# High part of the attention probabilities from a second exponential of the scores, not from a copy

## The chip, the cores and the metric

The kernel runs on one core of a Trainium2 chip. The time is device time in microseconds (us) for one execution, on inputs and outputs in device memory. A core has five engines that work at the same time, each on its own queue of instructions, in order: TensorE (PE, matmuls; PEld are its weight loads), VectorE (DVE), ScalarE (ACT, functions such as the exponential, and copies), GpSimd (POOL) and SyncE (SP, which starts most of the transfers). Matmul results land in PSUM, eight banks of 128 x 512 floats; POOL's operands here lie in SBUF.

## The reference

One layer of a decoder trunk over L = 1040 tokens (16 meta tokens and 1024 of the sequence), width 1024. An input projection feeds four mixers (pooling, attention, two convolutions), their outputs are gated, added and projected. Attention, which the change touches, has 8 heads, keys of 96 and values of 64:

```python
h = rms_norm(h_res, pre_norm_g[i])
z = h @ w_in[i]
...
s = jnp.einsum('bqhd,bkhd->bhqk', qb, k).astype(jnp.float32)
s = jnp.where(k_pos[None, :] <= q_pos[:, None], s, -jnp.inf)
p = jax.nn.softmax(s, axis=-1).astype(v.dtype)
return jnp.einsum('bhqk,bkhd->bqhd', p, v)
...
m = (gts[:, :, 0] * y_a + gts[:, :, 1] * y_b + gts[:, :, 2] * y_c + gts[:, :, 3] * y_d)
h_res = h_res + rms_norm(m @ w_o[i], post_norm_g[i])
```

## The kernel before

**Three-term products.** A float32 product is made of three matmuls in the format fp32r: each operand is split into a high part (the value rounded to fp32r) and a low part (the rest), and high x high, high x low and low x high are added in PSUM. The helper `split` (line 498) makes both parts: ACT copies the source into the high part, POOL subtracts the high part from the source to get the low one.

**Stages.** The first stage (to about 638 us) makes the input projection and the mixers' inputs. The second (638 to 838 us) is attention, mixed with the output products of the three other branches, which the code calls fills. The third makes the attention branch's output product and the last projection.

**Attention.** `attend(h, c)` (line 1507) works on one head `h` and one half `c` of the queries (512 of them). It runs over tiles of 128 keys, 4 full ones for `c = 0` and 8 for `c = 1`, and a last one of 16 keys. A tile covers 512 queries, or at the diagonal 400, 272, 144 and 16; over all heads 48 tiles have 512 columns, and 16 each have 400, 272 and 144. For each full tile:

- three matmuls into `s`, a PSUM bank of the tag `s`; five banks serve all users of that tag. Their rows read `ps_s<-qt,kt`;
- at the diagonal DVE adds a mask to the bank (`ps_s<-ps_s,maskT`);
- ACT takes the exponential into `p32` in SBUF, of which there are three buffers (`p<-ps_s`; a row maximum is already folded into the scores by four extra rows of the keys and queries);
- `split` makes `pt`, high and low side by side, four buffers (`pt<-p` on ACT, `pt<-p,pt` on POOL);
- three matmuls with the values add to `po`, the one bank `ps_o`: high x high, then the low part, then the third with the values' low part, which is put off by some tiles (`thirds`). A `pt` buffer is free after its third matmul.

The tile of 16 keys goes another way: ACT copies `p32` twice into `pz`, and POOL subtracts. At the end of a half ACT copies `po` to `ol` in SBUF (two buffers, one for a head); a new head's `ol` can be written when both products `op<-ol,rb` on DVE have read the one before the last. `rb` holds the reciprocal row sums, brought round by three small transfers; in the last head TensorE makes them by transposes (`ps_s<-ident,ol` and `ps_s<-ident,lcp`). POOL then multiplies with a gate (`op<-op,smg`), and `split` makes `boM` from it.

Two other users of the five banks and of TensorE stand between: the row maxima of a later half (`ps_s<-kt,qt`, masked with `maskS` and reduced on DVE into `mxs`), and the fills, six matmuls `ps_y<-bo,whl` each, of which DVE multiplies the result with a gate (`th<-th,ps_y`) and adds it up (`m<-m,th`, by turns on POOL).

**What sets the order.** Engine calls in the code don't issue anything. `Plan.record` notes each with its operands and a cost from a formula, and `Plan.flush` (line 364) runs a list scheduler over them: at each step an engine takes the noted instruction of lowest priority number that is ready and for which buffers are free. It then issues all instructions in the order found, from line 362, which is why every row of the profile names that one line. So the order on each engine, and which buffer a tile gets, is fixed ahead of time. A change in one instruction's operands or cost moves others in the stage.

Of the kernel before, what the change touches and what calls it, by code (L numbers as in the profile page):

```python
# [24 lines left out]
AF = mybir.ActivationFunctionType  # L25
# [8 lines left out]
NM = 16  # L34
# [38 lines left out]
def f(ap):  # L73
    return ap.bitcast(F32)
# [397 lines left out]
def trunk_kernel(ctx, tc, a):  # L472
    nc = tc.nc
    plan = Plan(nc)
    PE, ACT, DVE, POOL, SP = (plan.engine(e) for e in ("PE", "ACT", "DVE", "POOL", "SP"))
# [10 lines left out]
    def copy(out, in_, scale=1.0):  # L486
        ACT.activation(out, in_, AF.Copy, scale=scale)

    def sub(eng, out, x, y):
        eng.tensor_tensor(out, x, y, op=ALU.subtract)  # L490

    def add(eng, out, x, y):
        eng.tensor_tensor(out, x, y, op=ALU.add)
# [4 lines left out]
    def split(hi, lo, src, eng=None):  # L498
        copy(hi, src)
        sub(eng or POOL, lo, src, f(hi))  # L500
# [55 lines left out]
    def bank(tag="x"):  # L556

        return psum.tile([P, 512], F32, tag=tag, bufs=2 if tag == "x" else 1, name=f"ps_{tag}")
# [948 lines left out]
    def attend(h, c):  # L1507

        q_, k_, v_ = qt[h, c], kt[h % 2], vt[h % 2]
        po = bank("o")  # L1510
        nj = 4 * c + 5
        thirds = []

        def rest(last=False):
            PE.matmul(*thirds.pop(0), start=False, stop=last, skip_group_check=True)

        for j in range(nj):
            lo_ = max(512 * c, P * j - NM)
            n = 512 * (c + 1) - lo_
            kn = P if j < nj - 1 else NM  # L1520
            ks = slice(P * j, P * j + kn)
            qs = slice(512 - n, 512)
            s = bank("s")[:kn, :n]
            PE.matmul(s, k_[:NA, 0, ks], q_[:NA, 0, qs], start=True, stop=False)
            PE.matmul(s, k_[:QK, 0, ks], q_[:QK, 1, qs], start=False, stop=False)
            PE.matmul(s, k_[:QK, 1, ks], q_[:QK, 0, qs], start=False, stop=True)
            d0 = P * j - NM
            dl, dh = max(d0, 512 * c, 0), min(d0 + P, 512 * (c + 1))
            if dh > dl:
                sd = s[:, dl - lo_:dh - lo_]  # L1530
                add(DVE, sd, sd, maskT[:kn, dl - d0:dh - d0])
            p32 = at.tile([P, 512], F32, tag="p32", bufs=3, name="p32")[:kn, :n]
            ACT.activation(p32, s, AF.Exp)
            o = po[:, lo_ - 512 * c:]
            if kn == NM:
                x = pz[(2 * h + c) % 3]
                copy(x[:NM], p32)
                copy(x[64:], p32)
                sub(POOL, x[32:32 + NM], p32, f(x[:NM]))
                PE.matmul(o, vs[h % 2][:, c], x, start=False, stop=False, skip_group_check=True)  # L1540
                rest(last=True)
            else:
                pt_ = at.tile([P, 2, 512], F32R, tag="pt", bufs=4, name="pt")[:, :, :n]
                split(pt_[:, 0], pt_[:, 1], p32)
                PE.matmul(o, v_[:, j, :P], pt_[:, 0], start=(j == 0), stop=False, skip_group_check=True)
                if j == nj - 2:
                    rest()
                PE.matmul(o, v_[:, j, :P], pt_[:, 1], start=False, stop=False, skip_group_check=True)
                thirds.append((o[:64], v_[:, j, P:], pt_[:, 0]))
                if j < nj - 4 or j == nj - 2:  # L1550
                    rest()
            yield
        if c == 0:
            ol[h] = at.tile([P, 2, 512], F32, tag="ol", bufs=2, name="ol")
        with plan.late(500 if h == H - 1 else 0):
            copy(ol[h][:, c], po)
# [114 lines left out]
    for i, (h, c) in enumerate(seq):  # L1671
        with plan.behind() if i else nullcontext():
            if i + 2 < len(seq):
                load_q(*seq[i + 2])
            if c == 0 and h + 1 < H:
                load_kv(h + 1)
                if i == 0:
                    with plan.behind():
                        load_v(1)
            if h % 2 and c == int(h < H - 1):  # L1680
                smg[h] = at.tile([P, NT], F32, tag="smg", name="smg")
                ld(smg[h], z_dram[f"mg{h // 2}"])
        for j, _ in enumerate(attend(h, c)):
            if c and j == 4 and h + 2 < H:
                load_k(h + 2, 0, CUT)
            units += 1
            lead_to(-1, min(5 + units * 10 / 14, 5 * (i + 3)))
            refill()
        lead_to(i + 1)

        with plan.ahead(300 if h == H - 1 else -450):
            if h == H - 1:
                head_out(h, c, sums_pe(h, c))
            elif c:
                for k, rb in enumerate(sums(h)):
                    head_out(h, k, rb)
# [247 lines left out]
```

## Time and profile before

| | |
|---|---|
| median of 3 runs | 969.21 us (969.03 to 969.52) |
| the profiled execution | 968.91 us |
| its span, first to last instruction | 967.1 us |
| mean granted TensorE clock | 0.997 |
| attention stage | 638 to 838 us |
| ACT busy in `p32`, `pt` and `pz` instructions | 102.66 us |
| POOL busy in the same | 106.51 us |

The profile is one execution, taken by the hardware profiler. A row of a timeline gives the start and the length in us, the engine, the line, the operation, output<-inputs by the program's names, the shape and a count; in brackets stands the idle time before it and what ended it. A row of a group gives the busy time, the mean length of one in ns, and the idle time before the group. A row of waits names who waited for whom: us in total, times, the longest. A row of windows gives a stretch with its length, then the busy time of each engine with its count of instructions, the TensorE clock, the share of the transfer engines and GB/s.

### The profile page before, as it was taken

What the parts mean: (1) busy time and instruction counts of PE and PEld (TensorE: products, weight loads), DVE (VectorE), ACT (ScalarE), POOL (GpSimd) and SP (SyncE); (2) the same over time, 40 slices, a digit from 0 to 9 for tenths busy, and PEclk for the clock granted to TensorE, in tenths of its full rate; (3) what the DMA queues carried; (4) which work ended last, traced back from release to release, by engine and by line L of the source; (5) the groups of instructions that cost most, each with busy time, mean ns of one, the idle gap of its engine ahead of it and who ended that gap; (6) DMA issues with size and microseconds to landing.
All of it is one profiled execution on the core that took longest, in us unless ns stands there. A gap on an engine that the chain in (4) does not pass through costs nothing.

```text
span 967.1 us, 15247 instructions
## 1 busy us (share of the span) xinstructions
PE 950.4 (98%) x5003; PEld 808.9 (84%) x5003; DVE 696.0 (72%) x1113; ACT 449.1 (46%) x914; POOL 678.0 (70%) x628
## 2 busy tenths in 40 slices
PE   8999999999999999999999999999999999999996
PEld 7999899889888887888888878888888788788885
DVE  5856959988779855544536768346778889799757
ACT  7743233444344455554444344366555555225622
POOL 5957555666576787896679679655567786647955
PEclk9999999999999999999999999999999999999998
DMA  8145566668787687787655688699899664783633
GB/s 258 45 126 144 167 198 213 216 196 270 231 265 255 205 248 214 220 255 216 195 168 169 205 268 276 208 318 262 272 221 297 175 187 132 272 267 95 211 113 142
DMA packets 136330, 203.03 MB, mean 210 GB/s; under 512 B 19672, under 2 KB 83159, under 8 KB 135483
## 3 DMA queue, kind: packets, MB, share of 16 engines
q1 hardware_dynamic: 127274, 185.28, 63.3%
q10 hardware_dynamic: 8656, 15.74, 4.4%
q0 software_dynamic: 320, 1.05, 0.3%
q8 instruction: 39, 0.64, 0.3%
q14 instruction: 41, 0.33, 0.1%
HBM read 129.11 MB, written 72.88 MB: 209 GB/s over the span
## 4 chain that ended last, share of the span: by engine, by line
PE 90%; POOL 3%; DVE 2%; issue 2%; ACT 1%; DMA 1%; DVEq 0%; SPq 0%; POOLq 0%; ACTq 0%
PE ps_pa L362 16%; PE ps_pb L362 16%; PE ps_pc L362 15%; PE ps_o L362 9%; PE ps_y L362 8%; PE ps_s L362 8%; PE ps_pd L362 7%; PE ps_u L362 7%; PE ps_x L362 5%; POOL S L362 1%; POOL lsq L362 1%; ACT junk L362 1%; DVE c L362 0%; DMA lacc<-acc 0%; POOL u L362 0%
## 5 line engine op out<-in xcount | busy, mean ns | idle before, releaser
L362 PE MATMUL ps_pb<-T,S 128*128 128x512 f32 (+2 forms) x792 | 172.0, 359 | 0.0
L362 PE MATMUL ps_pa<-B,A 128*128 128x512 f32 (+2 forms) x792 | 171.7, 360 | 0.0
L362 POOL TENSOR_TENSOR A<-raw,A 128x512 fp32r<-128x512 f32 x84 | 114.3, 1368 | 61.3 <-ACT A L362 47.7
L362 PEld LDWEIGHTS ps_pb<-T,S 128*128 128x128 f32 x792 | 134.3, 189 | 22.4 <-issue 1.2
L362 PEld LDWEIGHTS ps_pa<-B,A 128*128 128x128 f32 x792 | 134.4, 188 | 22.3 <-issue 1.0
L362 POOL TENSOR_TENSOR S<-ss,S 128x512 fp32r<-128x512 f32 x84 | 116.0, 1393 | 51.8 <-ACT S L362 51.7
L362 POOL TENSOR_TENSOR pt<-p,pt 128x512 fp32r<-128x512 f32 (+1 forms) x96 | 102.8, 1094 | 52.5 <-PE ps_s L362 32.6
L362 DVE TENSOR_TENSOR u<-ps_pb,u 128x512 f32<-128x512 f32 (+2 forms) x66 | 40.3, 610 | 87.4 <-PE ps_pb L362 84.3
L362 DVE SCALAR_TENSOR_TENSOR ps_w<-conv,par,ps_w 128x512 f32<-128x512 f32 x116 | 87.1, 751 | 2.3
L362 PE MATMUL ps_y<-bo,whl 128*128 128x512 f32 x288 | 85.7, 403 | 0.9 <-DVE th L362 0.9
L362 PE MATMUL ps_pc<-B,S 128*128 128x512 f32 (+1 forms) x396 | 85.8, 358 | 0.0
L362 ACT ACTIVATE S<-ss 128x512 fp32r<-128x512 f32 x84 | 50.4, 627 | 74.5 <-DVE ss L362 43.7
L362 PE MATMUL ps_pd<-T,A 128*128 128x512 f32 (+2 forms) x396 | 84.9, 359 | 0.0
L362 PE MATMUL ps_pc<-T,S 128*128 128x512 f32 (+1 forms) x396 | 84.4, 359 | 0.0
L362 ACT ACTIVATE p<-ps_s 128x512 f32<-128x512 f32 (+4 forms) x112 | 49.7, 444 | 60.3 <-PE ps_s L362 29.2
L362 PEld LDWEIGHTS ps_pc<-T,S 128*128 128x128 f32 x396 | 66.8, 188 | 11.2 <-issue 0.7
L362 PEld LDWEIGHTS ps_pd<-T,A 128*128 128x128 f32 x396 | 67.1, 189 | 10.7
L362 PEld LDWEIGHTS ps_pc<-B,S 128*128 128x128 f32 x396 | 66.4, 189 | 10.2
L362 PE MATMUL ps_o<-pt,vt 128*128 128x512 f32 (+7 forms) x288 | 68.7, 346 | 0.2 <-ACT ol L362 0.2
L362 PE MATMUL ps_s<-qt,kt 100*128 100x512 f32 (+4 forms) x336 | 67.8, 324 | 0.0
L362 PEld LDWEIGHTS ps_s<-qt,kt 100*128 100x128 f32 (+1 forms) x336 | 54.1, 176 | 10.3 <-DVE qt L362 0.6
L362 ACT ACTIVATE A<-raw 128x512 fp32r<-128x512 f32 x84 | 52.0, 626 | 22.3 <-PE ps_pd L362 9.7
(281 smaller groups left out, 1890.4 us busy)
## 6 DMA issues: line engine op xcount, KB each, us to landing
raw<-in_w_in_dram SPq DMA_DIRECT2D x52, 512.0 KB
th<-th SPq DMA_DIRECT2D x32, 512.0 KB
th<-z ACTq DMA_DIRECT2D x60, 256.0 KB
v<-vhl SPq DMA_DIRECT2D x16, 384.0 KB
qt<-q SPq DMA_DIRECT2D x16, 384.0 KB
vt<-v SPq DMA_DIRECT2D x8, 768.0 KB
bo<-bo SPq DMA_DIRECT2D x6, 1024.0 KB
w_out_mla<-whl SPq DMA_DIRECT2D x16, 256.0 KB
```

The source lines that it names most:

```text
L362: getattr(self.handle[o["eng"]], o["op"])(*map(real, o["args"]), **{k: real(v) for k, v in o["kw"].items()})
```

## The change

For full tiles the high part of `pt` is no longer a copy of `p32`. ACT takes the exponential of the scores twice, both times from PSUM: first into the high part of `pt`, rounded to fp32r on writing, then into `p32`. POOL subtracts as before. The tile of 16 keys is as it was.

```diff
             p32 = at.tile([P, 512], F32, tag="p32", bufs=3, name="p32")[:kn, :n]
-            ACT.activation(p32, s, AF.Exp)
+            if kn == NM:
+                ACT.activation(p32, s, AF.Exp)
             o = po[:, lo_ - 512 * c:]
...
             else:
                 pt_ = at.tile([P, 2, 512], F32R, tag="pt", bufs=4, name="pt")[:, :, :n]
-                split(pt_[:, 0], pt_[:, 1], p32)
+                ACT.activation(pt_[:, 0], s, AF.Exp)
+                ACT.activation(p32, s, AF.Exp)
+                sub(POOL, pt_[:, 1], p32, f(pt_[:, 0]))
                 PE.matmul(o, v_[:, j, :P], pt_[:, 0], start=(j == 0), stop=False, skip_group_check=True)
```

The planner's order is the same up to the first attention tile and differs from there on. Three places follow. Numbers behind a name tell one buffer's use from another's; they differ between the two programs.

TensorE at the first scores of the stage, before and then now (`ps_s` scores, `ps_o` outputs with the values):

```order
L362 MATMUL ps_s_6902<-qt_6854,kt0_6865 128x144 x3
L362 MATMUL ps_s_6910<-qt_6854,kt0_6865 16x16 x3
L362 MATMUL ps_s_6918<-qt_6877,kt0_6865 128x512 x3
L362 MATMUL ps_o_6933<-pt_6916,vt0_6875 128x512
L362 MATMUL ps_s_6938<-qt_6877,kt0_6865 128x512 x3
L362 MATMUL ps_s_6947<-kt1_6867,qt_6880 128x144
```

```order
L362 MATMUL ps_s_6902<-qt_6854,kt0_6865 128x144 x3
L362 MATMUL ps_s_6910<-qt_6854,kt0_6865 16x16 x3
L362 MATMUL ps_o_6918<-pt_6907,vt0_6875 128x512
L362 MATMUL ps_s_6929<-qt_6877,kt0_6865 128x512 x3
L362 MATMUL ps_s_6940<-qt_6877,kt0_6865 128x512 x3
L362 MATMUL ps_o_6918<-pt_6907,vt0_6875 128x512
```

The first output matmul has moved ahead of the sixth tile of scores.

The second half of head 5 (of 0 to 7); its first scores come at about 761 us. TensorE, before and then now (`kt0_6865,qt` is a row-maximum tile):

```order
L362 MATMUL ps_y_8647<-bo_7470,whl_8214 128x512 x3
L362 MATMUL ps_s_8664<-qt_8199,kt1_6867 16x16 x3
L362 MATMUL ps_s_8675<-kt0_6865,qt_8534 128x328
L362 MATMUL ps_o_8678<-pt_8592,vt1_6904 128x512 x2
L362 MATMUL ps_o_8678<-pt_8592,vt1_6904 64x512
```

```order
L362 MATMUL ps_y_8629<-bo_7474,whl_8221 128x512
L362 MATMUL ps_o_8654<-pt_8584,vt1_6904 128x512 x2
L362 MATMUL ps_o_8654<-pt_8584,vt1_6904 64x512
...
L362 MATMUL ps_o_8654<-pt_8627,vt1_6904 128x512
L362 MATMUL ps_s_8681<-ident_62,mr_8664 4x128
L362 MATMUL ps_s_8683<-qt_8205,kt1_6867 16x16 x3
```

The outputs of three tiles and of part of a fourth now stand ahead of the 16-column scores. DVE at the same place, before and then now:

```order
L362 TENSOR_REDUCE mxs_6922<-ps_s_8568 128x1
L362 TENSOR_TENSOR ps_s_8570<-ps_s_8570,maskS_6857 128x128
...
L362 TENSOR_TENSOR ps_s_8629<-ps_s_8629,maskT_6861 128x128
L362 TENSOR_TENSOR op_8279<-ol_7956,rb_8497 64x512
L362 TENSOR_TENSOR op_8294<-ol_7956,rb_8497 64x512
```

```order
L362 TENSOR_REDUCE mxs_6921<-ps_s_8568 128x1
L362 TENSOR_TENSOR op_8159<-ol_7973,rb_8468 64x512
L362 TENSOR_TENSOR op_8282<-ol_7973,rb_8468 64x512
L362 TENSOR_TENSOR ps_s_8614<-ps_s_8614,maskT_6861 128x112
L362 TENSOR_TENSOR ps_s_8622<-ps_s_8622,maskT_6861 128x128
```

Both `op` products have moved ahead of the mask additions of this half. ACT's copy `ol`, which stood behind the exponentials of the fifth and the sixth tile there, now stands behind the fourth tile's.

ACT in the second half of the last head (first scores at about 811 us), before and then now (`ps_s_9229` is the fourth tile's bank in both, `ps_s_9239` the fifth's):

```order
L362 ACTIVATE p32_9267<-ps_s_9229 128x512
L362 ACTIVATE pt_9271<-p32_9267 128x512
L362 ACTIVATE p32_9280<-ps_s_9239 128x512
L362 ACTIVATE ol_9288<-ps_o_9118 128x512
L362 ACTIVATE p32_9295<-ps_s_9245 128x400
L362 ACTIVATE p32_9313<-ps_s_9252 128x272
L362 ACTIVATE pt_9320<-p32_9280 128x512
```

```order
L362 ACTIVATE pt_9265<-ps_s_9229 128x512
L362 ACTIVATE p32_9274<-ps_s_9229 128x512
L362 ACTIVATE p32_9279<-ps_s_9239 128x512
L362 ACTIVATE p32_9290<-ps_s_9247 128x400
L362 ACTIVATE p32_9299<-ps_s_9253 128x272
L362 ACTIVATE ol_9302<-ps_o_9108 128x512
L362 ACTIVATE boM20_9312<-op_8960 128x512
L362 ACTIVATE pt_9322<-ps_s_9239 128x512
```

The copy `ol` has moved behind the exponentials of the sixth and the seventh tile. On POOL two `op` products and one `boM` now stand ahead of the fifth tile's low part, where one `op` product stood.

## The prediction

> **What bounds the kernel now.** First the page, to see which engine is full.
>
> ```profile
> span 967.1 us, 15247 instructions
> PE 950.4 (98%) x5003; PEld 808.9 (84%) x5003; DVE 696.0 (72%) x1113; ACT 449.1 (46%) x914; POOL 678.0 (70%) x628
> ```
>
> TensorE (PE) is busy in 98% of the span. The change touches ScalarE (ACT), busy in 46%. So I cut out the attention stage, 638 to 838 us, and read there what TensorE waited for. The first row gives the span of the stretch and the busy time of PE, PEld (weight loads), DVE, ACT and POOL; the second is the same for the stage behind it, and the last row is from the chain of waits in that stage.
>
> ```profile
> 638.00:838.00 200.00, 197.89 (x1059) 164.07 (x1058) 159.01 (x357) 115.04 (x264) 137.32 (x139) 1.00 0.80 232
> 838.00:937.00 99.00, 99.00 (x438) 81.89 (x437) 80.85 (x89) 42.17 (x80) 68.35 (x46) 1.00 0.57 189
> PE ps_s L362 <- ACT p L362: 1.0, 1, 1.0
> PE ps_y L362 <- DVE th L362: 0.9, 1, 0.9
> PE ps_o L362 <- ACT ol L362: 0.2, 1, 0.2
> PEld ps_s L362 <- ACT p L362: 1.9, 4, 1.1
> 838.08 43.57 PE ps_u L362 x192
> ```
>
> TensorE is idle for 2.1 us of these 200: once for an exponential, once for a product of the branch work (`th`), once for the copy `ol`. Those few waits are all that faster attention could give back. A busy PE need not be a full one, so I checked the pace: in the last row 192 matmuls of 512 columns follow each other in 43.57 us, 226.9 ns each, with nothing between them.
>
> By the Trainium skill (Perfetto Trace Analysis, "Identifying the Most-Contended Engine") matmul busy time does not measure headroom, and the busy share of weight loads does. That is 164.07 of 200 here, so 35.9 us of the stage would be open. The trace speaks against it: in the 99 us from 838 to 937, where matmuls go at 226.9 ns, weight loads are busy for 81.89 us, the same 83%. It stays as a rival with a small chance.
>
> **The change part by part.** *ACT time.* For each of 96 tiles of scores ACT did an exponential from PSUM (`p<-ps_s`) and a copy of it from SBUF (`pt<-p`). Now it does two exponentials from PSUM. The groups by shape:
>
> ```profile
> L362 ACT ACTIVATE pt<-p 128x512 fp32r<-128x512 f32 x48 | 30.3, 632 | 2.6 <-PE ps_o L362 1.4
> L362 ACT ACTIVATE p<-ps_s 128x512 f32<-128x512 f32 x48 | 28.2, 588 | 34.6 <-PE ps_s L362 29.2 <-DVE ps_s L362 4.0 <-POOL pt L362 0.7
> L362 ACT ACTIVATE pt<-p 128x400 fp32r<-128x400 f32 x16 | 8.6, 536 | 0.4
> L362 ACT ACTIVATE p<-ps_s 128x400 f32<-128x400 f32 x16 | 8.0, 497 | 4.8 <-POOL pt L362 4.7
> L362 ACT ACTIVATE pt<-p 128x272 fp32r<-128x272 f32 x16 | 6.9, 429 | 0.4
> L362 ACT ACTIVATE p<-ps_s 128x272 f32<-128x272 f32 x16 | 6.2, 389 | 3.3 <-DVE ps_s L362 2.0 <-POOL pt L362 1.3
> L362 ACT ACTIVATE pt<-p 128x144 fp32r<-128x144 f32 x16 | 5.2, 324 | 0.5
> L362 ACT ACTIVATE p<-ps_s 128x144 f32<-128x144 f32 x16 | 4.6, 288 | 12.3 <-DVE ps_s L362 7.7 <-POOL pt L362 4.0 <-DVE mr L362 0.5
> ```
>
> The saving is 48 x 44 + 16 x 39 + 16 x 40 + 16 x 36 ns, 3.9 us of ACT's 115. TensorE hides it, except in the waits named above, so the term is 0. No row has an exponential that writes fp32r from PSUM. Its nearest rows are the 588 ns and, above, the 632 ns of the copy; at 632 the saving falls to zero, still hidden. TensorE, VectorE (DVE) and GpSimd (POOL) do the same instructions as before.
>
> *What is ready when.* For 512 columns the high part is there 632 ns earlier (no copy in front). The low part needs 588 + 588 ns of ACT instead of 588 + 632, so it gains 44 ns. The PSUM bank of the scores is freed 588 ns later, behind the second exponential. And a high part now needs its `pt` buffer (four of them, freed by TensorE) before the bank can be freed, where an exponential into one of three `p32` buffers was enough. Queued behind a late ACT instruction are the next exponentials and the copy `ol` that frees the accumulator `ps_o`; TensorE waits for those. So the change moves three or four waits of about 1 us, by the order that the planner now writes. I follow them by place.
>
> *The first scores (640 us).* In time order (start, length, engine, operation):
>
> ```profile
> 638.11 3.15 PE L362 MATMUL ps_s<-qt,kt 100*128 100x512 f32 x18
> 639.67 0.57 ACT L362 ACTIVATE p<-ps_s 128x512 f32<-128x512 f32 x1
> 640.27 0.63 ACT L362 ACTIVATE pt<-p 128x512 fp32r<-128x512 f32 x1
> 641.35 0.53 PEld L362 LDWEIGHTS ps_s<-qt,kt 100*128 100x128 f32 x3 [0.21 <-ACT p L362]
> 642.21 0.19 PEld L362 LDWEIGHTS ps_s<-kt,qt 96*128 96x128 f32 x1 [0.32 <-ACT p L362]
> ```
>
> Five tiles fill the five banks by about 640.1; the sixth waited until 640.3 for the bank of the first, the seventh and the next 0.21 and 0.32 us. Now the first output matmul stands ahead of the sixth tile. It starts at 639.67 + 0.59 + 0.06 = 640.3, a wait of 0.2, and ends at 640.55. The bank is free at 639.67 + 2 x 0.59 + 0.07 = 640.9, a wait of 0.4; the sixth tile ends at 641.6, and the second tile's two exponentials (0.50 each, from the groups) at 641.9, a wait of 0.3. That is 0.9 where there was about 0.6 to 0.7: +0.3 us, between 0 (the early output matmul fills it) and 0.9 (none of the old waits goes).
>
> *The stall at 768 us.*
>
> ```profile
> 763.54 0.43 DVE L362 TENSOR_REDUCE mxs<-ps_s 128x1 f32<-128x264 f32 x1
> 763.65 1.30 POOL L362 TENSOR_TENSOR pt<-p,pt 128x512 fp32r<-128x512 f32 x1 [5.10 <-ACT pt L362]
> 767.02 2.68 DVE L362 TENSOR_TENSOR op<-ol,rb 64x512 f32<-64x512 f32 x2
> 767.41 3.41 POOL L362 TENSOR_TENSOR pt<-p,pt 128x512 fp32r<-128x512 f32 x2
> 768.56 0.23 PE L362 MATMUL ps_s<-qt,kt 100*16 100x16 f32 x3
> 769.18 0.50 ACT L362 ACTIVATE p<-ps_s 128x400 f32<-128x400 f32 x1 [1.09 <-POOL pt L362]
> 769.73 0.60 ACT L362 ACTIVATE ol<-ps_o 128x512 f32<-128x512 f32 x1
> 769.74 0.42 PE L362 MATMUL ps_s<-kt,qt 96*128 96x328 f32 x1 [0.95 <-ACT p L362]
> 770.38 0.48 PEld L362 LDWEIGHTS ps_o<-pt,vt 128*128 128x128 f32 x3 [0.46 <-ACT ol L362]
> ```
>
> TensorE finishes the 16-column scores at 768.8, waits until 769.74 for a bank (the exponential waits for `p32`, held by late POOL subtractions), and until 770.38 for `ol`, which waited for the DVE products until 769.7: 0.95 + 0.46, about 1.5 us with the weight loads. In the new order both `op` products stand right behind the row maximum that ended at 764.0, before the mask additions, so at up to 1.34 us each (2.68 / 2) they end by 766.7. `ol` stands ahead of the fifth exponential, and output matmuls stand ahead of the 16-column scores and the row-maximum tile. TensorE then has work there: -1.5 us, with 0 as the other bound, if POOL's two subtractions (3.41 / 2 = 1.7 us each) make the outputs wait instead.
>
> *The last long half (819 us).* The same kind of wait turns up here.
>
> ```profile
> 813.51 6.06 POOL L362 TENSOR_TENSOR pt<-p,pt 128x512 fp32r<-128x512 f32 x4 [4.82 <-PE ps_s L362]
> 817.21 0.60 ACT L362 ACTIVATE ol<-ps_o 128x512 f32<-128x512 f32 x1
> 818.36 0.51 ACT L362 ACTIVATE p<-ps_s 128x400 f32<-128x400 f32 x1 [0.56 <-POOL pt L362]
> 818.93 0.32 PEld L362 LDWEIGHTS ps_s<-ident,ol 64*128 64x128 f32 x4 [0.35 <-ACT p L362]
> 819.32 2.35 PE L362 MATMUL ps_o<-pt,vt 128*128 128x512 f32 x9
> 819.52 1.76 POOL L362 TENSOR_TENSOR op<-op,smg 128x512 f32<-128x512 f32 x1
> 819.60 0.40 ACT L362 ACTIVATE p<-ps_s 128x272 f32<-128x272 f32 x1 [0.73 <-POOL pt L362]
> ```
>
> `ol` was done at 817.8, behind the fifth exponential. Now it stands behind the seventh (272 columns), which gets its `p32` when the fourth subtraction ends, 813.51 + 6.06 = 819.57. So `ol` runs from 820.0 to 820.6, and the outputs that need its bank start at 820.7. TensorE comes there at 818.93 + 2 x 0.227 = 819.4 (two branch matmuls now stand ahead): a wait of 1.3 us. Behind it two POOL instructions more stand ahead of the fifth low part: after 819.57 come two `op` products (1.76 each), `boM` and the low part (1.30 each), to 825.7. TensorE, late itself and with 21 matmuls (some 4.7 us) from 820.7 up to it, wants it at 825.4. So +1.3 us; bounds 0 (the four subtractions take 1.30 us each, as the one at 763.65 did, 0.9 us less in all, and ACT gets through sooner) and 2.0 (each low part late as well).
>
> *The end of the branch work (835 us).*
>
> ```profile
> 834.47 1.29 DVE L362 TENSOR_TENSOR op<-ol,rb 64x512 f32<-64x512 f32 x2
> 836.41 1.67 PE L362 MATMUL ps_y<-bo,whl 128*128 128x512 f32 x6 [0.91 <-DVE th L362]
> ```
>
> Two `op` products stand in a row before the `th` product that frees a bank; one of them now stands earlier. That takes 1.29 / 2 = 0.65 off a 0.91 us wait; as two bank products stay in a row I take -0.4, between -0.9 and 0.
>
> *The other halves.* There are 16 halves of heads. Banks held 588 ns longer cost something where a tile comes soon after its bank is freed. Four weight loads waited for such a bank, 1.9 us in all; I put the new ones at +0.4, between 0 and 16 x 0.59 = 9.4.
>
> The sum: 0 + 0.3 - 1.5 + 1.3 - 0.4 + 0.4 = +0.1 on the profiled execution's 968.91 us (its span of 967.1 and 1.8 around it). The median of the runs shown is 969.21, 0.3 above. I forecast **969.0 us**, no measurable change.
>
> **The rivals.**
> (1) *Banks held longer decide.* In eight halves (the second of each head) nine tiles share five banks and four `pt` buffers; from the fifth tile on a bank is freed only when TensorE has used an older `pt`. If the planner's order leaves less than two exponentials (1.2 us) between a bank's last matmul and its next, TensorE pays the longer hold: 8 x 0.59 = 4.7 us, 969.0 + 4.7 - 0.4 (the allowance above) = 973.3. For it: 819 us, and exponentials already wait for POOL. Against it: ACT was idle for 34.6 us before its 512-column exponentials, 29.2 of it for TensorE's scores, so it mostly keeps up.
> (2) *The old stalls go and none comes.* 968.9 - 1.5 - 0.9 = 966.5. For it: high parts 632 ns earlier, `op` products earlier. Against it: the `ol` order at 819.
> (3) *It does not do what it says.* High parts come earlier, but the order, written ahead of time, uses them no earlier, and every wait stays: 968.9.
> (4) *TensorE is not full*, by the row on weight loads. ACT's 3.9 us and the earlier high parts shorten the stage: 965.0. The 226.9 ns speak against it.
>
> **How the numbers follow.** Forecast 0.58, (1) 0.20, (2) 0.10, (3) 0.10, (4) 0.02. A measurement tells about 0.2%, 1.9 us, from no change. Forecast and (3) lie within it, (1) is slower, (2) and (4) faster: faster 0.12, same 0.68, slower 0.20. The forecast's own range, with one or two places at a bound, is 967.5 to 970.9. For 8 in 10, I leave out (4), most of (2), and the half of (1) beyond four halves (2.4 us and some): 967.1 to 972.2.
>
> **What would show it.** ACT's `pt<-ps_s` and `p<-ps_s` at about 588 ns for 512 columns, ACT's busy time in the stage near 111; waits for ACT near 640 of about 0.9 us; none at 768; about 1.3 us for `ol` near 819 (this place decides between forecast and (2)); a wait for `th` near 835 of about 0.5. I am wrong if TensorE's idle time in the stage goes beyond 4 us, or if ACT's new instruction takes well over 632 ns.

## The result, and the profile after

The changed kernel takes **972.64 us** (median of 6 runs, 971.89 to 974.02) against 969.22 us before (6 runs, 968.91 to 969.52). The ratio is 1.0036, 95% interval 1.0026 to 1.0046: 3.4 us slower, beyond the forecast of 969.0 and just beyond its range. Four of the six runs lie between 971.9 and 972.9 us, two at 974; the profiled one is the fastest, 971.89 us.

From the page and the windows of the changed kernel (span of the stretch, then busy time of PE, PEld, DVE, ACT and POOL, the clock, the transfer share and GB/s):

```profile
PE 952.0 (98%) x5003; PEld 810.0 (84%) x5003; DVE 689.4 (71%) x1113; ACT 439.4 (45%) x914; POOL 674.5 (70%) x628
638.00:841.00 203.00, 198.31 (x1057) 164.12 (x1056) 158.13 (x356) 105.94 (x265) 140.29 (x142) 1.00 0.76 232
```

The attention stage, from the first matmul of scores to the first `ps_u`, grew from 199.8 to 203.1 us; what follows it is 0.7 us shorter. ACT has 9.1 us less to do in the stage (115.04 before), yet TensorE now stands for 4.7 us of it, where it stood for 2.1. Who held it, from the list of waits in that stretch:

```profile
PE ps_y L362 <- DVE th L362: 2.8, 3, 1.4
ACT ol L362 <- DMA th<-zlast: 1.9, 1, 1.9
PE ps_o L362 <- ACT ol L362: 1.3, 1, 1.3
PE ps_s L362 <- DVE qt L362: 0.4, 1, 0.4
PEld ps_s L362 <- ACT p L362: 0.6, 2, 0.3
```

PE's wait for an exponential (`ps_s <- ACT p`, 1.0 us before) is gone, and of the weight loads' waits for one 0.6 us are left of 1.9; those that came are for VectorE and, by way of `ol`, for a transfer. To place them I took the starts of successive matmuls and counted what lies between two beyond the usual interval of that shape (227 ns for 512 columns). All such stalls over 0.15 us, in us, by the time in the changed kernel:

| place | before | changed kernel | what TensorE waits for now |
|---|---|---|---|
| 640, first scores | 0.17 | 0.43 | first `pt`, then a bank |
| 646, first copy `ol` | 0 | 1.47 | `ol`, which waits for the transfer `th<-zlast` |
| 653 | 0 | 0.28 | the low part of `pt` from POOL |
| 664 | 0 | 0.60 | `qt` on DVE |
| 768 to 773 | 1.59 | 0.17 | |
| 788 | 0 | 0.23 | `pz` from POOL |
| 820, last long half | 0 | 1.62 | `th` on DVE |
| 836 to 839 | 1.09 | 1.72 | `th` on DVE |
| sum | 2.9 | 6.5 | |

The largest new one is at 646 us, a place that the prediction didn't name. The rows there in time order, first of the kernel before, then of the changed one:

```profile
640.05 0.54 POOL L362 DMA_DIRECT2D th<-zlast  x1 [2.88 <-ACT zlast L362]
640.30 0.32 SPq L362 DMA_DIRECT2D qt<-q  x1
640.66 0.90 SPq L362 DMA_DIRECT2D bo<-bo  x2
645.70 0.59 ACT L362 ACTIVATE ol<-ps_o 128x512 f32<-128x512 f32 x1
```

```profile
637.10 0.34 SPq L362 DMA_DIRECT2D bo<-bo  x1
640.18 0.54 POOL L362 DMA_DIRECT2D th<-zlast  x1 [2.88 <-ACT zlast L362]
640.43 0.33 SPq L362 DMA_DIRECT2D qt<-q  x1
647.34 0.60 ACT L362 ACTIVATE ol<-ps_o 128x512 f32<-128x512 f32 x1 [1.91 <-DMA th<-zlast]
647.99 0.50 PE L362 MATMUL ps_o<-pt,vt 128*128 128x512 f32 x1 [1.31 <-ACT ol L362]
```

`zlast` is a tile of the first stage, and `ol` lies partly on its place in SBUF, in both kernels. Before, both loads `bo<-bo` (1024 KB each by the view of transfers) stood behind the load of `qt` in SP's queue, which waits for a buffer until 640.3 us. In the new order one of them stands ahead of it and goes out 3 us before POOL's last store of `zlast`. The view of transfers gives that store's time to landing, before and after:

```profile
th<-zlast POOLq DMA_DIRECT2D x1, 256.0 KB, 4.6
```

```profile
th<-zlast POOLq DMA_DIRECT2D x1, 256.0 KB, 7.1
```

The stall at 820 us, in time order:

```profile
817.21 1.72 DVE L362 TENSOR_TENSOR op<-ol,rb 64x512 f32<-64x512 f32 x1
819.05 1.57 DVE L362 TENSOR_TENSOR op<-ol,rb 64x512 f32<-64x512 f32 x1
820.66 0.60 ACT L362 ACTIVATE ol<-ps_o 128x512 f32<-128x512 f32 x1
820.74 0.69 DVE L362 SCALAR_TENSOR_TENSOR th<-th,ps_y 128x512 f32<-128x512 f32 x1
821.49 0.73 PE L362 MATMUL ps_y<-bo,whl 128*128 128x512 f32 x2 [1.45 <-DVE th L362]
```

`ol` ran from 820.66 to 821.26, where the prediction had 820.0 to 820.6. But the wait that ended last was the branch product `th`, behind two products of head 5 on DVE. And at the end of the branch work, before and after:

```profile
833.03 0.69 DVE L362 TENSOR_TENSOR m<-m,th 128x512 f32<-128x512 f32 x1
835.68 0.67 DVE L362 SCALAR_TENSOR_TENSOR th<-th,ps_y 128x512 f32<-128x512 f32 x1
```

```profile
834.53 1.34 DVE L362 TENSOR_TENSOR m<-m,th 128x512 f32<-128x512 f32 x1
835.88 0.68 DVE L362 TENSOR_TENSOR op<-ol,ps_s 64x512 f32<-64x512 f32 x1
836.58 0.68 DVE L362 TENSOR_TENSOR op<-ol,rb 64x512 f32<-64x512 f32 x1
837.18 0.67 DVE L362 SCALAR_TENSOR_TENSOR th<-th,ps_y 128x512 f32<-128x512 f32 x1
837.91 1.66 PE L362 MATMUL ps_y<-bo,whl 128*128 128x512 f32 x6 [1.14 <-DVE th L362]
839.82 1.42 PE L362 MATMUL ps_y<-bo,whl 128*128 128x512 f32 x5 [0.25 <-DVE th L362]
```

Two products still stand in a row ahead of `th`, where three stood before (from 833.75 us). But the sum `m<-m,th` ahead of them takes 1.34 us instead of 0.69.

### The profile page after: what moved, and what is told of

Same layout as the page of the kernel before. It is cut to its first block, busy times and chain, and to the rows that moved or that the text cites. A ratio compares the mean times of both kernels' runs of the same rounds, so it can differ in the third digit from the quotient of the medians.

```text
span 969.7 us, 15172 instructions
## 1 busy us (share of the span) xinstructions
PE 952.0 (98%) x5003; PEld 810.0 (84%) x5003; DVE 689.4 (71%) x1113; ACT 439.4 (45%) x914; POOL 674.5 (70%) x628
## 4 chain that ended last, share of the span: by engine, by line
PE 90%; POOL 3%; DVE 3%; issue 2%; DMA 2%; ACT 1%; DVEq 0%; SPq 0%; POOLq 0%; ACTq 0%
PE ps_pa L362 16%; PE ps_pb L362 16%; PE ps_pc L362 15%; PE ps_o L362 10%; PE ps_u L362 8%; PE ps_pd L362 7%; PE ps_y L362 7%; PE ps_s L362 7%; PE ps_x L362 5%; POOL S L362 1%; DMA th<-zlast 1%; POOL lsq L362 1%; DMA lacc<-acc 0%; DVE m L362 0%; DVE th L362 0%
## 5 line engine op out<-in xcount | busy, mean ns | idle before, releaser
L362 PE MATMUL ps_y<-bo,whl 128*128 128x512 f32 x288 | 87.8, 404 | 2.8 <-DVE th L362 2.8
L362 ACT ACTIVATE pt<-ps_s 128x512 fp32r<-128x512 f32 (+1 forms) x96 | 48.8, 509 | 58.9 <-PE ps_s L362 30.7
```

The lines of the kernel that those rows point to most:

```text
L362: getattr(self.handle[o["eng"]], o["op"])(*map(real, o["args"]), **{k: real(v) for k, v in o["kw"].items()})
```

## The experiments

The theory: the change of instruction does little harm; the order that the planner writes around it does, by a few waits with names. The rival: banks that are held for a second exponential cost the time. For the runs below the issue loop takes the planner's list and changes only what is shown, so every other instruction keeps its place on its engine. Each was timed against the kernel before on the same chip; that one's medians there were 969.39, 969.84 and 969.54 us for the first, second and third group of four. The groups ran on different chips, so between groups the distance from the kernel before is the better measure; for the changed kernel it is 3.4 us.

| run | median us (runs) | ratio to before, 95% |
|---|---|---|
| old_order_exp | 972.39 (11) | 1.0026 (1.0018 to 1.0035) |
| new_order_copy | 973.93 (5) | 1.0045 (1.0033 to 1.0058) |
| after_ol_moved | 970.38 (11) | 1.0009 (1.0000 to 1.0018) |
| after_products_later | 975.80 (5) | 1.0062 (1.0048 to 1.0076) |
| after_bo_later | 970.34 (11) | 1.0009 (1.0000 to 1.0018) |
| products_earlier | 970.69 (11) | 1.0010 (1.0001 to 1.0019) |
| products_both | 968.37 (11) | 0.9986 (0.9977 to 0.9995) |
| before_ol_moved | 969.78 (11) | 1.0003 (0.9994 to 1.0012) |
| after_all | 968.04 (11) | 0.9981 (0.9973 to 0.9990) |
| after_all_copy | 971.30 (11) | 1.0019 (1.0011 to 1.0028) |
| before_two_moves | 974.70 (6) | 1.0046 (1.0033 to 1.0060) |
| old_exp_products | 970.12 (11) | 1.0007 (0.9999 to 1.0016) |

**Order and instruction apart (old_order_exp, new_order_copy).** One kernel has the old order with the new instruction, the other the new order with the old one. At issue:

```diff
+        o = self.swap.get(o["i"], o) if "i" in o else o
...
                 split(pt_[:, 0], pt_[:, 1], p32)
+                hi = plan.ops[-2]
+                plan.swap[hi["i"]] = {**hi, "args": (pt_[:, 0], s, AF.Exp), "kw": {}}
```

```diff
                 sub(POOL, pt_[:, 1], p32, f(pt_[:, 0]))
+                hi, p_ = plan.ops[-3:-1]
+                plan.swap[hi["i"]] = {**p_, "i": hi["i"]}
+                plan.swap[p_["i"]] = {**hi, "args": (pt_[:, 0], p32, AF.Copy), "kw": {"scale": 1.0}}
```

> Every engine issues in the order of the kernel before, instruction for instruction; only the content of 93 of the 96 copies is the second exponential (3 stay copies, where the bank's next tile is issued ahead of it). So the banks are held longer and ScalarE does the new work, but nothing is moved. Theory 1 (the new order and the waits in it cost the 3.4 us): 969.2, between 968.5 and 970.0, ScalarE's busy time in the stage some 8 us less than before. Theory 2 (banks that are held for a second exponential, or the exponential itself, cost it): 972 to 973. Between the two, 970.0 to 971.5, each has a part.

> Every engine issues in the order of the changed kernel, but in 95 of the 96 tiles the first of the two ScalarE instructions is the plain exponential and the second is the copy of it, as in the kernel before, so that the bank is free after the first. Theory 1 (the order): 972.6, between 971.5 and 974. Theory 2 (held banks or the instruction): about 969.2. A middle result gives each its part.

Neither theory is right as it stood: 972.39 and 973.93 us, both slower than before. The new order costs 4.5 us with copies, and with copies it is slower than with the second exponential. The old order with the second exponential split into two groups: four runs at 970.2 to 971.1 us with a mean granted clock of 0.997, which is 0.8 to 1.7 us over the kernel before, and seven at 972.4 to 973.5 with 0.995 or 0.996. The profiled run is one of the seven. Its rows at the place of the old stall, and the windows around it (the last three figures are the clock, the transfer share and GB/s):

```profile
768.88 3.59 DVE L364 TENSOR_TENSOR op<-ol,rb 64x512 f32<-64x512 f32 x2
772.50 0.60 ACT L364 ACTIVATE ol<-ps_o 128x512 f32<-128x512 f32 x1 [1.72 <-DVE op L364]
773.15 1.11 PE L364 MATMUL ps_o<-pt,vt 128*128 128x512 f32 x2 [1.90 <-ACT ol L364]
```

```profile
772.00:774.00 2.00, 0.85 (x2) 0.62 (x3) 1.94 (x4) 0.89 (x2) 2.00 (x2) 0.83 0.15 53
774.00:776.00 2.00, 2.00 (x6) 1.44 (x5) 1.97 (x5) 1.15 (x2) 1.27 (x2) 0.50 0.43 103
776.00:778.00 2.00, 2.00 (x9) 1.44 (x9) 0.47 (x1) 1.44 (x4) 2.00 (x3) 0.82 0.98 267
```

Two products that took 2.68 us here before take 3.59 us and start 1.9 us later. Most of the 1.9 us isn't theirs: the `th` ahead of them, at 756.44 us before, already runs 1.75 us late, at 758.19. `ol` waits for the products, TensorE for `ol`, 2.17 us by the starts of its matmuls. Then its clock is at half: matmuls of 512 columns follow each other at 430 ns instead of 227. The lost share of the clock is 2 x (0.17 + 0.50 + 0.18) = 1.7 us.

**The same with the products earlier (old_exp_products).** Old order, second exponential, and on DVE the two products of head 3 among the three masks ahead of them:

```diff
+            rest = [o for o in dve[at - 3:dve.index(first[1])] if o not in first]
+            dve[at - 3:dve.index(first[1]) + 1] = [first[0], *rest[:2], first[1], *rest[2:]]
```

> old_order_exp (972.4: seven runs at 972.4 to 973.5 with a mean granted clock of 0.995 or 0.996, four at 970.2 to 971.1 with 0.997) with one move: the two products of head 3 among the three masks ahead of them. Theory (there the products run 1.9 us later than before and stretch to 3.6 us, ol waits for them, TensorE stands 2.2 us, and then in some runs its clock falls to 0.5 for some 3 us): the stall near 771 us falls under 1 us, the clock is 0.997 in nearly all runs, and the time is 969.5 to 970.3; what is left over 969.5 is the price of the held banks. Rival (the held banks themselves hold that place): a stall of over 1.5 us stays and the runs still split into two groups.

970.12 us. No run has a clock below 0.997, and only one is above 970.5. The pair of stalls at 770 us is 1.56 us in all, no longer 2.49. So the group at 973 came from that stall. What is left stands where banks are reused soonest: stalls of 0.65, 0.31 and 0.50 us at 640, 647 and 657 us, where the kernel before has 0.17. In these stalls the held banks cost about 1.3 us. What they cost in the time isn't shown as well: the median is 0.6 us over the kernel before, the interval reaches from nothing to 1.6 us (0.9999 to 1.0016), and this run has the products moved as well.

**The wait at 646 us, by two ways (after_ol_moved, after_bo_later, before_ol_moved).** First `ol` gets another place, the order untouched; then the place stays, and two neighbours in SP's queue change places.

```diff
-    for n, tag in ((2, 'ol'),):
+    for n, tag in ((1, 'rb'), (1, 'op0'), (1, 'op1')):
         at.tag(tag, n)
```

```diff
+        sp = [o for o in order if o["eng"] == "SP"]
+        k = next((k for k, o in enumerate(sp) if o["i"] == self.bo), None)
+        if k is not None:
+            sp[k], sp[k + 1] = sp[k + 1], sp[k]
```

> The changed kernel with the same order on every engine; only the place of the tile ol in SBUF is exchanged with that of rb, op0 and op1 (8 KB each way), so that the first copy out of ps_o no longer lies on the tile zlast, from which a DMA is still reading. Theory 1 with the wait for that DMA as one of its parts: the stall of 1.47 us near 646 us goes, 972.6 becomes about 971.2 and the runs spread less than 971.9 to 974.0, since the landing of one DMA no longer sets the time. If the stall is only taken over by another wait right behind it (theory 2, something else bounds this place): 972.6 as it is.

> The changed kernel with two neighbours exchanged in SyncE's order and nothing else: the first load bo<-bo stands behind the load of qt, as in the kernel before, no longer ahead of it. Theory: in the changed kernel this 512 KB load goes out 3 us before the last store th<-zlast (637.10 against 640.18 us) and that store then takes 7.1 us to land, where it took 4.6 us with the load behind it, and this is why the first copy ol waits. Then here the store lands in about 4.7 us, ol waits for no DMA, the stall near 646 us is under 0.3 us, and the time is 970.0 to 970.8 with no run near 974. Rival (the late landing is chance, or comes from something else in the new order): the store lands in 6.5 to 7.5 us and the time stays at 972 to 974.

> The kernel before with the same exchange of places in SBUF as in the run after_ol_moved, with its order as it was. Theory: here the last store th<-zlast had landed before the first copy ol, so the exchange has nothing to take away: 969.2, within 0.5 us. Rival (the place of ol costs both kernels the same, and the difference of the changed kernel is elsewhere): about 967, the 2 us that the exchange took off the changed kernel.

Both take 2.3 us off the changed kernel, 970.38 and 970.34 us (1.0 and 0.5 us over the kernel before, where the changed kernel was 3.4), and of their 22 runs none is above 971.5. The profile of after_ol_moved, its slowest run, has a stall of 1.2 us in place of that one, at 661 us, where TensorE waits for another load on SP's queue, `qt<-q`; the one of after_bo_later has none there. In after_bo_later the store of `zlast` lands sooner (the view of transfers), and `ol` is back at 645.47 us without a wait (in time order):

```profile
th<-zlast POOLq DMA_DIRECT2D x1, 256.0 KB, 4.9
```

```profile
640.50 0.32 SPq L363 DMA_DIRECT2D qt<-q  x1
640.86 0.91 SPq L363 DMA_DIRECT2D bo<-bo  x2
645.47 0.60 ACT L363 ACTIVATE ol<-ps_o 128x512 f32<-128x512 f32 x1
```

Over all fourteen profiles the store took 4.6 to 5.7 us to land with both loads behind it (eight), and 6.7 to 7.5 us with one ahead (six). The kernel before gained nothing from the other place of `ol` (969.78 against 969.84): there the store had landed in time. The step is shown: one load moved ahead of another in SP's queue. (The load is of 1024 KB, not of 512 as the expectation has it.)

**The stall at 820 us (after_products_later, products_earlier).** First the products of head 5 go behind the branch products on DVE, then ahead of where they were.

```diff
+        if h == H - 3:
+            plan.moved.add(len(plan.ops) - 1)
...
+            sts = [x for x in range(k, min(k + 12, len(dve))) if dve[x]["op"] == "scalar_tensor_tensor"][:2]
+            if sts:
+                dve.insert(sts[-1] + 2, o)
+                dve.remove(o)
```

```diff
+            rest = [o for o in dve[a:dve.index(first[1])] if o not in first]
+            dve[a:dve.index(first[1]) + 1] = [first[0], *rest[:2], first[1], *rest[2:]]
```

> The changed kernel with one thing moved: on VectorE the two products op<-ol,rb of head 5 stand behind the next two products th<-th,ps_y and their sums, no longer ahead of them. Theory 1 with VectorE's order as the cause of the stall of 1.62 us near 819.6 us: that stall goes and 972.6 becomes about 971.0. Rival (that stall is the long half being fed too late, and the copy ol would hold TensorE there anyway): 972.2 to 972.6, with a stall of 1 us or more left near 820 that waits for ol or pt.

> The changed kernel with ol moved in SBUF (970.4), and on VectorE the two products op<-ol,rb of head 5 three and two instructions earlier: the first ahead of the three masks, the second behind the second mask, where the kernel before has them. Moving them back behind the branch products made the stall at 820 us longer (1.6 to 3.1 us), for the copy ol of head 7 waited for their end. Theory (these products are late, and both ol and the branch products behind them wait): the stall near 819 us falls from 1.6 to under 0.4 us and the time from 970.4 to about 969.0. Rival (TensorE is fed late at this place by the tiles pt or the masks, that now wait instead): the stall stays over 1 us with another releaser, and the time at 970 or above.

Later was wrong, and plainly: the stall grew from 1.62 to 3.13 us.

```profile
823.66 1.29 DVE L363 TENSOR_TENSOR op<-ol,rb 64x512 f32<-64x512 f32 x2
824.98 0.60 ACT L363 ACTIVATE ol<-ps_o 128x512 f32<-128x512 f32 x1 [2.81 <-DVE op L363]
825.63 0.73 PE L363 MATMUL ps_o<-pt,vt 128*128 128x512 f32 x2 [2.97 <-ACT ol L363]
```

I had taken the products for bystanders in DVE's queue. But they also free the buffer that `ol` of head 7 needs, since `ol` has two buffers. In this profile the wait at 646.7 us is 1.93 us, and behind it the clock falls as above:

```profile
650.00:652.00 2.00, 2.00 (x10) 1.79 (x9) 1.25 (x4) 2.00 (x5) 2.00 (x3) 0.57 1.01 404
652.00:654.00 2.00, 2.00 (x8) 1.56 (x7) 0.84 (x4) 1.12 (x3) 2.00 (x2) 0.58 1.05 276
```

Earlier, with `ol` at its other place, was no gain either: 970.69 us, in place of after_ol_moved's 970.38, 0.9 and 1.0 us over the kernel before. The stall at 818 us fell to 1.17 us, and 0.40 us came at 828.6. The rows of the next run, with the same place, say why.

**The end of the branch work too (products_both).** As products_earlier, and the last products of heads 6 and 7 behind the next two branch products.

```diff
+        if h >= H - 2 and c:
+            plan.moved.add(len(plan.ops) - 1)
```

> As products_earlier, and the last two products of heads 6 and 7 (second half) also moved, behind the next two branch products instead of ahead of them. If the stalls of 1.3 and 0.4 us near 836 and 839 us are only this order: both fall under 0.3 us together and the time is about 967.6. If VectorE is the bound of these last 10 us (about 2 us of its work for each branch product and sum beside GpSimd, against 2.7 us of TensorE's for two): the stalls move behind, and the time is that of products_earlier within 0.5 us. If the last tile boM comes too late: a stall appears behind 841 us instead.

968.37 us: the stalls of 1.3 and 0.4 us near 836 and 839 us are gone and nothing came behind them. They were order alone. At 818 us:

```profile
818.76 0.40 ACT L367 ACTIVATE p<-ps_s 128x272 f32<-128x272 f32 x1 [0.75 <-POOL pt L367]
819.06 0.59 ACT L367 ACTIVATE ol<-ps_o 128x512 f32<-128x512 f32 x1
819.70 2.13 PE L367 MATMUL ps_o<-pt,vt 128*128 128x512 f32 x8 [1.00 <-ACT ol L367]
```

With `th` out of the way, TensorE waits for `ol`, and `ol` for the seventh tile's exponential and its `p32` buffer: the prediction's mechanism, hidden until now behind another.

**All of it, with exponentials and with copies (after_all, after_all_copy).** On top of products_both: the load of `bo` behind that of `qt`, `ol` of head 7 two places earlier on ACT, the last `pz` subtraction one place earlier on POOL. The second kernel has the same order with copies.

```diff
+            if (h, c) == (H - 1, 0):
+                plan.up["ACT", 2] = len(plan.ops) - 1
...
+                if (h, c) == (H - 1, 1):
+                    plan.up["POOL", 1] = len(plan.ops) - 1
```

> products_both (968.4) with three neighbours' exchanges more: the first load bo<-bo behind that of qt on SyncE; the first copy ol of head 7 two places earlier on ScalarE, ahead of the exponentials p<-ps_s that wait for a buffer p32; the last small subtraction pz one place earlier on GpSimd, ahead of boM. Theory (the stall of 1.17 us near 818.3 us is ol in ScalarE's queue behind those exponentials, the one of 0.4 us near 828.8 us is pz behind boM on GpSimd): both stalls go, 968.4 becomes 966.9. Rival (the branch products or pt hold TensorE there next): a stall of over 0.6 us stays near 818 to 821 us and the time at 967.7 or above.

> The order of after_all on every engine, but in 95 of the 96 tiles the plain exponential comes first and the copy of it second, as in new_order_copy against the changed kernel. If the second exponential is worth something in an order that suits it (the high part is there after one ScalarE instruction, not two, and successive exponentials overlap): 1.0 to 1.5 us slower than after_all, as new_order_copy is 1.3 us slower than the changed kernel (973.9 against 972.6). If what counts is the order alone: the same as after_all within 0.4 us. If the held banks cost something here: faster than after_all.

968.04 us, 0.9981 of the kernel before (0.9973 to 0.9990): the fastest here, but a miss by 1.1 us. `pz` is settled, `ol` runs at 816.45 us, and a third wait takes its place:

```profile
820.57 0.63 ACT L367 ACTIVATE boM<-op 128x512 fp32r<-128x512 f32 x1 [1.31 <-POOL op L367]
821.11 0.58 ACT L367 ACTIVATE pt<-ps_s 128x512 fp32r<-128x512 f32 x1
821.74 0.46 PE L367 MATMUL ps_s<-ident,ol 64*128 64x64 f32 x4 [1.07 <-ACT pt L367]
```

This one is a held bank. The fifth tile's second instruction stands on ACT behind `boM`, which waits for POOL, and only behind it is the bank free. With copies the same order takes 971.30 us, 3.3 us more. So in this order the second exponential is worth something. That it is worth 3.3 us in the best order for each is not shown, since this order was made for the exponentials.

**The same moves in the kernel before (before_two_moves).** Copies, old order, products of head 3 among the masks, the last products later.

```diff
+        if h == 3:
+            plan.early.add(len(plan.ops) - 1)
+        if h >= H - 2 and c:
+            plan.moved.add(len(plan.ops) - 1)
```

> The kernel before, with copies, and only two moves on VectorE: the two products of head 3 among the three masks that stood ahead of them, and the last products of heads 6 and 7 behind the next two branch products. If the gain of products_both over the kernel before is nothing but VectorE's order, it is there for the copies too: the stalls of 1.1 and 0.5 us near 769 us and of 1.1 us near 835 us go, and 969.5 becomes 967.0 to 967.6. If the old order needs its products where they are (a mask that comes later holds the exponentials): 969 or above.

974.70 us, a miss. The stalls at 769 us did not go: they are 1.83 us in all, where the kernel before has 1.59. And the last tile `boM` now comes too late for the third stage:

```profile
842.62 0.63 ACT L363 ACTIVATE boM<-op 128x512 fp32r<-128x512 f32 x1 [3.96 <-POOL op L363]
844.31 4.03 PE L363 MATMUL ps_u<-boM,whl 128*128 128x512 f32 x10 [2.68 <-POOL boM L363]
```

The clock fell twice, behind the stalls at 769 and 841 us. The move that took 2.3 us off products_earlier (970.69 to 968.37) makes a stall of 2.85 us here: in the old order these products already stood one branch product further on.

## Why the prediction was wrong

- **ACT time, 0.** Right that it is hidden, wrong in size: 9.1 us less in the stage, not 3.9. The new instruction takes 612 ns for 512 columns, not 588, but starts 0.48 us behind the last (see the end).
- **The first scores, +0.3.** Right by the stalls over 0.15 us (0.43 where 0.17 was), and near in that by luck: it reckoned with 0.9 and 0.6 to 0.7. With all shorter ones counted as well, TensorE lost 0.8 us up to 643 us in both kernels, so the term may be 0, its lower bound.
- **The stall at 768 us, -1.5.** Right in size: 1.59 us became 0.17. Of the two reasons given (products ahead of the masks, output matmuls to do) the first isn't enough: with the products among the masks the old order keeps 1.56 us (old_exp_products) and 1.83 us (before_two_moves). The second is left, and no run tried it alone.
- **The last long half, +1.3.** Right in size (1.62) and half right in cause. `ol` did stand behind the seventh exponential, and held TensorE for 1.17 us once `th` was moved. But DVE's products held `th` until the same time. Three waits lie on top of each other there; taking away one and then another left 1.17 and 1.25 us.
- **The end of the branch work, -0.4.** Wrong in sign: +0.6 (1.72 against 1.09). The step counted the product that had moved away and not what else stands on DVE: the sum `m<-m,th` ahead of the products took 1.34 us, not 0.69, and ate up the 0.65 that the product had cost. So `th` follows the `th` before it by 3.33 us, and by 3.37 in the kernel before. It ran 1.5 us later than before, at 837.18 us, while TensorE came to it only 1.3 us later, and behind the next sum, of 1.27 us, a second wait of 0.4 us came. products_both shows that the order sets it.
- **The other halves, +0.4.** This is the step that failed most: 1.47 + 0.28 + 0.60 + 0.23 = 2.6 us. It priced banks alone ("Banks held 588 ns longer cost something"), and none of the four stalls is a bank: the larger part, 1.47 us, comes from a load on SP's queue, the others wait for POOL or DVE. The prediction followed four engines by place and never compared SP's order, though its first difference, at 637.1 us, comes ahead of the first scores of the stage. after_bo_later shows 2.3 us from this exchange.

The terms above, measured, come to +3.7 us against a stage that is 3.3 us longer, and the sign that the prediction set itself came: TensorE stood for more than 4 us of the stage (4.7). The median has 0.75 us over the profiled run, the fastest of the six. Two of the six came at 974 us, with a mean clock of 0.996. That their clock fell behind the wait for `zlast`, as in after_products_later, fits (without the wait, 22 runs have none such), but neither of the two was profiled.

The rival (1), held banks at 973.3 us, came near in its number and not by its mechanism: in the changed kernel only the second part of the stall at 640 us is a bank (0.26 us), in the old order held banks cost about 1.3 us of stalls (old_exp_products), and with the bank freed after the first instruction the new order is slower still (973.93). The rival (2), the old stalls gone and none come, was never far: it took another order, after_all, to get most of the way (968.04 against its 966.5). Rival (3) fell with the moved stalls. For rival (4) nothing speaks: the busy time of weight loads is the same (164.07 and 164.12 us) in a longer stage; the share before was 82%, not the 83% that the prediction read.

## What to carry to other kernels

Where a list scheduler writes the order, compare every queue, the one that only starts transfers first: a load moved ahead of another can delay a store on a different queue and through it a buffer. Before moving an instruction that seems in the way, list all that waits for it, its buffer included, and expect a second wait under the first; a stall is worth what is left when it goes, not its length. And judge a change in such a kernel with the order held fixed, both ways round.

## What the runs showed of the hardware

**Two exponentials take less time than their lengths add up to.** ACT in the changed kernel, and in the kernel before, in time order:

```profile
813.07 0.60 ACT L362 ACTIVATE pt<-ps_s 128x512 fp32r<-128x512 f32 x1 [3.98 <-PE ps_s L362]
813.56 0.59 ACT L362 ACTIVATE p<-ps_s 128x512 f32<-128x512 f32 x1
814.04 0.60 ACT L362 ACTIVATE pt<-ps_s 128x512 fp32r<-128x512 f32 x1
```

```profile
813.28 0.58 ACT L362 ACTIVATE p<-ps_s 128x512 f32<-128x512 f32 x1
813.90 0.63 ACT L362 ACTIVATE pt<-p 128x512 fp32r<-128x512 f32 x1
814.44 0.58 ACT L362 ACTIVATE p<-ps_s 128x512 f32<-128x512 f32 x1
```

Starts are 0.49 and 0.48 us apart at a length of 0.60, so neighbours overlap by some 0.11 us. A copy of the exponential just made starts 0.62 us behind it: it has to wait for its end. A tile takes 0.97 us of ACT instead of 1.16. The Trainium skill (ScalarE: Activation LUTs, "What ACT_TABLE_LOAD costs") has back-to-back ACTIVATEs overlap by about 93 ns, which these rows bear out, with 0.11 us, for instructions that don't read each other's result.

**A stall of some 2 us can cost 1.7 us more, through the clock.** Behind stalls of 1.9 us (after_products_later, at 647 us) and 2.2 us (old_order_exp, at 771 us) TensorE ran at half its clock, and lost 1.7 us each time: 2 x (0.43 + 0.42) in the first. In before_two_moves the same came behind 1.8 us in two pieces (at 769 us) and behind 2.85 us (at 841 us). Each of the four stretches has a clock of 0.50 for 3.4 us, from 650.3 to 653.7 us in the first. It is not certain to come: in the same profile of after_products_later a stall of 3.1 us at 822 us had no such effect, the kernel before kept its clock behind 1.59 us in two pieces, and four of eleven runs of old_order_exp kept theirs. By the Trainium skill (TensorE: Matmul & The Clock Gate, "Part 1: The HAM clock gate (the "warmup" mystery)") the clock is halved after an idle window of about 3.4 us that runs freely. A halved stretch of 3.4 us agrees with that; that it comes behind a stall of 1.9 us, shorter than that window, and not always behind one of 3.1, is what the runs add.

**Some instructions on VectorE take longer while GpSimd works, others don't.** Over all fourteen profiles, the DVE instructions of 512 columns that read SBUF alone, `m<-m,th` and `op<-ol,rb`, took 0.68 to 0.70 us in all 198 rows in which POOL stood idle. In the 273 rows in which POOL was busy all through, 249 took more than 0.75 us, up to 1.91. Those that read one operand from PSUM, `th<-th,ps_y` and `op<-ol,ps_s`, took 0.62 to 0.69 us in all 476 rows, whatever POOL did. Why is not shown. So a place on DVE has no fixed price: the sum of 1.34 us at 834.53 ran beside a POOL instruction (834.02 to 835.31 us), the one of 0.69 us in the kernel before beside none.

**A load on one queue can delay a store on another.** POOL's last store of `zlast`, 256 KB, took 4.6 to 5.7 us to land, and 6.7 to 7.5 us with a load of 1024 KB issued on SP's queue 2.5 to 3.2 us ahead of it.
